# Adaptive max pooling over 8192 rows: a nine-row ring, long load runs, and all stores behind all loads on GpSimd's queue

## The chip, the cores and the metric

The kernel runs on one core of one Trainium2 chip. The metric is the device time of an execution in microseconds (us). A time given as a median is that of several executions; a span is the time from the first to the last instruction of the one execution that the profiler recorded, and is a little shorter than that execution's own time.

## The reference

The input `x` has 32 x 256 x 4096 float32 values, 134.2 MB. Each row of 4096 values is cut into 256 windows of 16, and the largest value of each window is kept. The output has 32 x 256 x 256 values, 8.39 MB.

```python
for i in range(output_size):                 # 256
    start = int(i * length / output_size)    # length 4096: windows of 16
    end = int((i + 1) * length / output_size)
    result[:, :, i] = np.max(x[:, :, start:end], axis=-1)
```

## The kernel before

The 32 x 256 rows are seen as 8192 rows of 16 KB. SBUF has 128 partitions, so 64 rows fall to each partition; below, "a row" of the kernel means one row in each of the 128 partitions, 2.1 MB in and 128 KB out. One instruction of VectorE, a `reduce_max` over the innermost axis, turns a row's 128 x 4096 values into 128 x 256.

**Body.** Two rows at a time are loaded (L80), so that a partition receives one contiguous run of 32 KB. `n_body` is 30 such tiles `t`, in a pool of three buffers (`IN_BUFS`). The loads are issued from SP's queue. Each tile is reduced by two instructions (L83) into an output tile `o` of 128 x 512. The first 14 output tiles are stored as soon as they are made, from ScalarE's queue (L92), in runs of 2 KB. The last 16 tiles of the body are put on a list, `deferred`.

**Tail.** `emit_deferred` (L75) issues stores off that list from SP's queue: six behind the last load of the body, five between the two single-row loads and the chunks, five at the end. Two further rows are loaded one by one (`tr`, L107), and the last two rows are loaded in four chunks each (`tl`, L118), runs of 4 KB, each reduced by its own instruction (L121). ScalarE stores the two output tiles of the tail (L127, L131).

The order of work is the program's order on each queue; the tile framework adds the waits. A load waits until the buffer that it is to fill has been reduced, and a reduction waits until its load has landed. SP works its list off in order, so whatever stands behind a waiting load waits too.

Of the kernel before, what the change touches and what calls it, by code (L numbers as in the profile page):

```python
# [1 line left out]

# [4 lines left out]


@with_exitstack  # L10
def kernel(
    ctx: ExitStack,
    tc: tile.TileContext,
    x: bass.AP,
    output_size: bass.AP,
    out: bass.AP,
):
    nc = tc.nc

    B, C, L = x.shape  # L20
    O = int(output_size)
    assert L % O == 0, (L, O)
    W = L // O

    P = nc.NUM_PARTITIONS

    xf = x.flatten_outer_dims()
    of = out.flatten_outer_dims()
    rows = xf.shape[0]
    assert rows % P == 0  # L30

    fp32 = mybir.dt.float32

    R = 2
    IN_BUFS = 3
    CHUNKS_PER_ROW = 4
    N_CHUNK_ROWS = 2
    N_FULL_ROWS = 2
    DEF_A = 6
    DEF_B = 5  # L40
    DEF_C = 5

    while R > 1 and rows % (P * R) != 0:
        R //= 2
    nprow = rows // P
    nmacro = nprow // R
    n_chunks = CHUNKS_PER_ROW if O % CHUNKS_PER_ROW == 0 else 1
    oc = O // n_chunks

    n_tail_prow = min(N_CHUNK_ROWS + N_FULL_ROWS, nprow)  # L50
    n_chunk_prow = min(N_CHUNK_ROWS, n_tail_prow)
    n_tail_macro = -(-n_tail_prow // R)
    n_body = nmacro - n_tail_macro
    tail_start_prow = n_body * R
    n_defer = min(DEF_A + DEF_B + DEF_C, max(n_body - 1, 0))

    xt = xf.rearrange("(n p r) (o w) -> n p r o w", p=P, r=R, w=W)
    ot = of.rearrange("(n p r) m -> n p (r m)", p=P, r=R)

    in_pool = ctx.enter_context(tc.tile_pool(name="inpool", bufs=IN_BUFS))  # L60
    out_pool = ctx.enter_context(
        tc.tile_pool(name="outpool", bufs=min(nmacro, n_defer + 5))
    )

    out_tiles = {}
    deferred: list[int] = []

    def new_out():
        return out_pool.tile([P, R * O], fp32, tag="out", name="o")

    def emit_deferred(k):
        for _ in range(k):
            if deferred:
                m = deferred.pop(0)
                nc.sync.dma_start(out=ot[m], in_=out_tiles[m])  # L75

    defer_start = n_body - n_defer
    for n in range(n_body):
        t = in_pool.tile([P, R, O, W], fp32, tag="in")
        nc.sync.dma_start(out=t, in_=xt[n])  # L80
        o = new_out()
        for r in range(R):
            nc.vector.reduce_max(  # L83
                out=o[:, r * O : (r + 1) * O],
                in_=t[:, r],
                axis=mybir.AxisListType.X,
            )
        out_tiles[n] = o
        if n >= defer_start:
            deferred.append(n)  # L90
        else:
            nc.scalar.dma_start(out=ot[n], in_=o)  # L92

    emit_deferred(DEF_A)

    o = None
    last_n = nmacro - 1
    for q in range(tail_start_prow, nprow):
        n, r = divmod(q, R)
        if r == 0 or o is None:  # L100
            o = new_out()
            out_tiles[n] = o
        if q == nprow - n_chunk_prow:
            emit_deferred(DEF_B)
        if q < nprow - n_chunk_prow:
            tr = in_pool.tile([P, 1, O, W], fp32, tag="inrow", bufs=2)
            nc.sync.dma_start(out=tr, in_=xt[n][:, r : r + 1])  # L107
            nc.vector.reduce_max(  # L108
                out=o[:, r * O : (r + 1) * O],
                in_=tr[:, 0],  # L110
                axis=mybir.AxisListType.X,
            )
        else:
            for c in range(n_chunks):
                tl = in_pool.tile(
                    [P, oc, W], fp32, tag="inchunk", bufs=2 * n_chunks
                )
                nc.sync.dma_start(  # L118
                    out=tl, in_=xt[n][:, r, c * oc : (c + 1) * oc, :]
                )  # L120
                nc.vector.reduce_max(  # L121
                    out=o[:, r * O + c * oc : r * O + (c + 1) * oc],
                    in_=tl,
                    axis=mybir.AxisListType.X,
                )
        if r == R - 1 and n != last_n:
            nc.scalar.dma_start(out=ot[n], in_=o)  # L127

    emit_deferred(len(deferred))

    nc.scalar.dma_start(out=ot[last_n], in_=out_tiles[last_n])  # L131


# [1 line left out]
_INS = ['x', 'output_size']  # L135
_OUTS = [((32, 256, 256), 'float32')]
#: Inputs that are plain numbers.
_NUMBERS = {'output_size': 256}


# [26 lines left out]
```

## Time and profile before

| | |
|---|---|
| median of 7 executions | 338.76 us (338.42 to 339.2) |
| the profiled execution's own time | 339.2 us |
| its span | 337.4 us |
| VectorE busy | 281.0 us, 70 instructions |
| one row's reduction (L83) | 4414 ns |
| VectorE's idle time before L83, ended by a load | 50.4 us |
| HBM read, written | 134.22 MB, 8.39 MB |
| moved over the span | 423 GB/s |
| DMA transfers | 30 of 4096 KB, 2 of 2048 KB, 8 of 512 KB, 32 stores of 256 KB |

The instruction rows of the profile give the engines' work; the DMA rows give what the 16 DMA engines did. A "packet" of the DMA rows is one contiguous run, as one of the engines moved it, or one of the tiny records with which a transfer reports that it has landed, 16 for each transfer. The share of a queue is the time that its packets took, over 16 engines' span.

### The profile page before, as it was taken

What the parts mean: (1) busy time and instruction counts of PE and PEld (TensorE: products, weight loads), DVE (VectorE), ACT (ScalarE), POOL (GpSimd) and SP (SyncE); (2) the same over time, 40 slices, a digit from 0 to 9 for tenths busy, and PEclk for the clock granted to TensorE, in tenths of its full rate; (3) what the DMA queues carried; (4) which work ended last, traced back from release to release, by engine and by line L of the source; (5) the groups of instructions that cost most, each with busy time, mean ns of one, the idle gap of its engine ahead of it and who ended that gap; (6) DMA issues with size and microseconds to landing.
All of it is one profiled execution on the core that took longest, in us unless ns stands there. A gap on an engine that the chain in (4) does not pass through costs nothing.

```text
span 337.4 us, 241 instructions
## 1 busy us (share of the span) xinstructions
DVE 281.0 (83%) x70; POOL 0.2 (0%) x4
## 2 busy tenths in 40 slices
DVE  0488988888988889888889888888998888899885
POOL 0000000000000000000000000000000000000000
DMA  8999999999999999999999999999999999999997
GB/s 315 435 435 454 404 454 409 450 412 450 418 441 434 426 436 421 458 400 458 404 436 435 435 435 435 435 435 435 431 435 435 435 431 435 417 395 430 400 388 279
DMA packets 10370, 142.63 MB, mean 423 GB/s; under 512 B 1152, under 2 KB 1152, under 8 KB 6272
## 3 DMA queue, kind: packets, MB, share of 16 engines
q1 hardware_dynamic: 8064, 138.42, 96.1%
q10 hardware_dynamic: 2304, 4.20, 3.2%
q14 instruction: 2, 0.02, 0.0%
HBM read 134.22 MB, written 8.39 MB: 423 GB/s over the span
## 4 chain that ended last, share of the span: by engine, by line
DMA 74%; DVE 24%; SPq 1%; issue 0%; DVEq 0%
DMA t<-in_x_dram 60%; DVE o L83 23%; DMA tl<-in_x_dram 7%; DMA out_dram<-o 7%; SPq L75 1%; DVE o L121 0%; SPq L80 0%; DVEq L83 0%
## 5 line engine op out<-in xcount | busy, mean ns | idle before, releaser
L83 DVE TENSOR_REDUCE o<-t 128x256 f32<-128x4096 f32 x60 | 262.4, 4414 | 50.4 <-DMA t<-in_x_dram 50.4
L121 DVE TENSOR_REDUCE o<-tl 128x64 f32<-128x1024 f32 x8 | 9.8, 1220 | 1.2 <-DMA tl<-in_x_dram 1.0
L108 DVE TENSOR_REDUCE o<-tr 128x256 f32<-128x4096 f32 x2 | 8.8, 4420 | 1.3 <-DMA tr<-in_x_dram 1.2
L148 POOL MEMSET const-bfloat16-1.0<- 128x1 bf16 x1 | 0.1, 102 | 0.0
L148 POOL MEMSET const-uint8-127<- 128x1 uint8 x1 | 0.1, 102 | 0.0
L148 POOL MEMSET const-float32-1.0<- 128x1 f32 x1 | 0.1, 99 | 0.0
L148 POOL MEMSET const-float32-0.0<- 128x1 f32 x1 | 0.1, 98 | 0.2 <-issue 0.2
## 6 DMA issues: line engine op xcount, KB each, us to landing
t<-in_x_dram SPq DMA_DIRECT2D x30, 4096.0 KB, 21.6
out_dram<-o ACTq DMA_DIRECT2D x16, 256.0 KB, 15.2
out_dram<-o SPq DMA_DIRECT2D x16, 256.0 KB, 14.3
tr<-in_x_dram SPq DMA_DIRECT2D x2, 2048.0 KB, 16.5
tl<-in_x_dram SPq DMA_DIRECT2D x8, 512.0 KB, 9.4
```

The source lines that it names most:

```text
L75: nc.sync.dma_start(out=ot[m], in_=out_tiles[m])
L83: nc.vector.reduce_max(out=o[:, r * O : (r + 1) * O], in_=t[:, r], axis=mybir.AxisListType.X,)
L108: nc.vector.reduce_max(out=o[:, r * O : (r + 1) * O], in_=tr[:, 0], axis=mybir.AxisListType.X,)
L121: nc.vector.reduce_max(out=o[:, r * O + c * oc : r * O + (c + 1) * oc], in_=tl, axis=mybir.AxisListType.X,)
L148: nc = _bacc.Bacc("TRN2", target_bir_lowering=False, num_devices=1)
```

## The change

The input comes through one tile, `ring`, of nine rows. `LOAD` is three: every load brings three rows, a run of 48 KB in each partition, into a third of the ring; there are 21 of them, and one load of a single row at the end. The rows are dealt out in three groups of `G` = 21 rows to a partition, so that a partition's 21 rows are contiguous in the input and in the output; the runs that the partitions load at one time are thus 336 KB apart. Every row has its own reduction into one of three output tiles of 21 rows (21 KB in each partition); they stay in SBUF until the loads are issued. The last row is reduced into a free part of the ring, `spare`.

After the last load the stores are issued: two whole groups (21 KB runs), the third in two pieces (`CUT`: 15 rows, 6 rows), and the last row's 1 KB runs.

The helper `move` picks the queue. The very first load is issued from SP. All other loads, and four of the five stores, are issued from GpSimd's queue with `single_packet=True`; the last row's store is issued from ScalarE. SP's queue thus holds one transfer, ScalarE's one, GpSimd's 25. On GpSimd's queue the order is: loads 2 and 3, which wait for nothing; loads 4 to 21 and the last row's, each of which waits for an earlier load and for VectorE; the stores of groups 1 and 2 without a wait of their own; the two stores of group 3, each with a wait for VectorE.

```diff
@@ -15,126 +14,78 @@
     output_size: bass.AP,
     out: bass.AP,
 ):
+
+
+
     nc = tc.nc
+    P = nc.NUM_PARTITIONS
+    fp32 = mybir.dt.float32
 
     B, C, L = x.shape
     O = int(output_size)
     assert L % O == 0, (L, O)
     W = L // O
-
-    P = nc.NUM_PARTITIONS
-
     xf = x.flatten_outer_dims()
     of = out.flatten_outer_dims()
     rows = xf.shape[0]
-    assert rows % P == 0
+    assert rows == 64 * P
 
-    fp32 = mybir.dt.float32
+    RING = 9
+    G = 21
+    N_GROUPS = 3
+    LOAD = 3
+    CUT = 15
 
-    R = 2
-    IN_BUFS = 3
-    CHUNKS_PER_ROW = 4
-    N_CHUNK_ROWS = 2
-    N_FULL_ROWS = 2
-    DEF_A = 6
-    DEF_B = 5
-    DEF_C = 5
+    pool = ctx.enter_context(tc.tile_pool(name="pool", bufs=1))
+    ring = pool.tile([P, RING, O, W], fp32, tag="ring", name="ring")
+    outs = [
+        pool.tile([P, G * O], fp32, tag=f"out{i}", name=f"out{i}")
+        for i in range(N_GROUPS)
+    ]
 
-    while R > 1 and rows % (P * R) != 0:
-        R //= 2
-    nprow = rows // P
-    nmacro = nprow // R
-    n_chunks = CHUNKS_PER_ROW if O % CHUNKS_PER_ROW == 0 else 1
-    oc = O // n_chunks
+    main = N_GROUPS * G * P
+    xg = xf[0:main].rearrange("(g p r) (o w) -> g p r o w", p=P, r=G, w=W)
+    og = of[0:main].rearrange("(g p r) m -> g p (r m)", p=P, r=G)
+    xl = xf[main:rows].rearrange("p (o w) -> p o w", w=W)
+    ol = of[main:rows]
 
-    n_tail_prow = min(N_CHUNK_ROWS + N_FULL_ROWS, nprow)
-    n_chunk_prow = min(N_CHUNK_ROWS, n_tail_prow)
-    n_tail_macro = -(-n_tail_prow // R)
-    n_body = nmacro - n_tail_macro
-    tail_start_prow = n_body * R
-    n_defer = min(DEF_A + DEF_B + DEF_C, max(n_body - 1, 0))
+    def pooled(dst, src):
+        nc.vector.reduce_max(out=dst, in_=src, axis=mybir.AxisListType.X)
 
-    xt = xf.rearrange("(n p r) (o w) -> n p r o w", p=P, r=R, w=W)
-    ot = of.rearrange("(n p r) m -> n p (r m)", p=P, r=R)
+    def move(dst, src):
+        if n_read == 0:
+            nc.sync.dma_start(out=dst, in_=src)
+        else:
+            nc.gpsimd.dma_start(out=dst, in_=src, single_packet=True)
 
-    in_pool = ctx.enter_context(tc.tile_pool(name="inpool", bufs=IN_BUFS))
-    out_pool = ctx.enter_context(
-        tc.tile_pool(name="outpool", bufs=min(nmacro, n_defer + 5))
-    )
+    n_read = 0
+    for g in range(N_GROUPS):
+        for r in range(0, G, LOAD):
+            at = n_read % RING
+            move(ring[:, at : at + LOAD], xg[g][:, r : r + LOAD])
+            for i in range(LOAD):
+                pooled(outs[g][:, (r + i) * O : (r + i + 1) * O], ring[:, at + i])
+            n_read += LOAD
 
-    out_tiles = {}
-    deferred: list[int] = []
+    at = n_read % RING
+    spare = ring[:, (at + LOAD) % RING].rearrange("p o w -> p (o w)")[:, 0:O]
+    move(ring[:, at], xl)
+    pooled(spare, ring[:, at])
 
...
+    for g in range(N_GROUPS - 1):
+        move(og[g], outs[g])
+    for a, b in ((0, CUT), (CUT, G)):
+        move(
+            og[N_GROUPS - 1][:, a * O : b * O],
+            outs[N_GROUPS - 1][:, a * O : b * O],
+        )
+    nc.scalar.dma_start(out=ol, in_=spare)
```

More of the change, by code (lines that the diff above doesn't have):

```diff
@@ L66 @@
-    deferred: list[int] = []
[L68 to L90, printed above, removed]
-        else:
-            nc.scalar.dma_start(out=ot[n], in_=o)
@@ L94 @@
[L94 to L127, printed above, removed]
@@ L129 @@
-    emit_deferred(len(deferred))
-    nc.scalar.dma_start(out=ot[last_n], in_=out_tiles[last_n])
+    assert rows == 64 * P
[12 more added lines that the diff above has]
+    xg = xf[0:main].rearrange("(g p r) (o w) -> g p r o w", p=P, r=G, w=W)
```

## The prediction

> **What bounds the kernel now.** I read the page's busy shares and DMA queues first, then the waits, then the DMA view in windows.
>
> ```profile
> span 337.4 us, 241 instructions
> DVE 281.0 (83%) x70; POOL 0.2 (0%) x4
> q1 hardware_dynamic: 8064, 138.42, 96.1%
> q10 hardware_dynamic: 2304, 4.20, 3.2%
> L83 DVE TENSOR_REDUCE o<-t 128x256 f32<-128x4096 f32 x60 | 262.4, 4414 | 50.4 <-DMA t<-in_x_dram 50.4
> ```
>
> The two queues' packets (SP is q1, ScalarE q10) took 99.3% of 16 engines' span: the 16 DMA engines are the bound. VectorE needs 4.41 us a row of tiles and all its 50.4 us of idle time at L83 ended with a load. A row is 2.10 MB, 4.85 us at the 432 GB/s that the table of windows gives for 14 to 300 us; so VectorE keeps pace with 9% to spare.
>
> Time can therefore come only from what DMA records cost, from gaps between them, and from the two ends. Three windows of the DMA view give the price of a record. 200 to 260 us (32 KB load records only), 309 to 315 (16 KB only), 60 to 70 (loads with ScalarE's 2 KB stores):
>
> ```profile
> q1 hardware_dynamic: 889, 25.99, 100.5%
> ...
> q1 hardware_dynamic: 174, 2.59, 101.2%
> ...
> q1 hardware_dynamic: 143, 4.16, 96.4%
> q10 hardware_dynamic: 143, 0.26, 6.8%
> ```
>
> Columns: packets, MB, share of 16 engines. Each transfer also has 16 tiny records (72 transfers, 1152 records under 512 B on the page). First line: 889 - 96 = 793 records in 0.1005 x 600 x 16 = 964.8 us, **1216 ns for 32 KB**. Second: 158 in 97.2 us, 615 ns for 16 KB. Fourth: 127 in 10.9 us less 0.1 for the tiny ones, 84.6 ns for 2 KB. The first and last give a line: **9.2 ns + 36.83 ns per 1000 B** (1131.4 ns over 30,720 B); it puts 16 KB at 612.6, near the measured 615. The tiny ones I take at the line's 9.2.
>
> The last two lines show also how two queues share an engine: 143 records each. They take turns one for one, whatever their size.
>
> Now add up the records of one engine (an eighth of 128 partitions' runs, 8 a transfer): 240 of 32 KB, 291.8; 16 of 16 KB, 9.8; 64 of 4 KB at 160, 10.2; 256 of 2 KB, 21.7; 72 tiny, 0.7. **Sum 334.2.** The DMA view shows the first bytes near 1.76 us and the last near 336.2, 1.2 before the end: 1.76 + 334.2 + 1.2 = 337.2 against 337.4. The kernel before is one unbroken row of records, its tail included.
>
> **What the Trainium skill says.** (1) "DMA: Bandwidth & Descriptors", Queues, rings and completion order: an engine goes round its queues packet by packet and drains a whole packet first. The trace agrees on turns, and shows 32 KB records of SP's queue as turns of their own; no packet of several records is in it. (2) Same page, Specifications: first byte some 1 us after issue from GpSimd, 0.6 from SP. SP's took 1.0 here (issue at 0.73). (3) "SBUF — State Buffer", Who interferes with whom: on trn2 a tensor_reduce never contends with GpSimd, so descriptors written by GpSimd aren't held up by VectorE. No run here shows it yet; I cost that contention at nothing. (4) First page again, Latency and other measured facts: engines 7 and 15 are usually slower, perhaps from GpSimd's descriptor rings. The trace, with no GpSimd DMA, can't say.
>
> **The change, part by part.** *Longer records.* An engine's loads become 21 x 8 = 168 records of 49,152 B at 9.2 + 1810.3 = 1819.5 ns, 305.7 us, and 8 of 16 KB, 4.9. The reader should see how little is to be had: bytes cost 36.83 either way, and 240 + 16 + 64 = 320 fixed parts become 176, 144 x 9.2 ns = 1.3 us. *Stores.* Two groups of 21,504 B a partition (801 ns), then 15,360 (575) and 6,144 (235.5), and the last row's 1,024 (46.9): 8 x 2459.4 ns = 19.7 us, for 21.7. *Fewer transfers:* 27 for 72, 0.25 for 0.66 us. **Sum 330.5, 3.7 less**, all of it on the bounding engines: -1.3 - 2.0 - 0.4.
>
> *The ring.* Nine rows in loads of three keep three loads in flight. In the order of instructions a load's reuse waits on VectorE and the earlier load only. Load k+3 can issue 13.24 us (3 x 4.414) after load k lands, while loads k+1 and k+2 hold the engines for 8 x 1819.5 = 14.56 us each. It is then queued 29.1 - 13.2 = 15.9 us ahead of need, less some 1.4 us for GpSimd's issue. Cost nothing, covered by those two loads. If the cover goes, the engines idle.
>
> *Issue from GpSimd.* All but two of 27 transfers go to POOL's queue, which had four memsets. SP keeps load 1, ScalarE the last row's store. Nothing else needs POOL. The trace has no GpSimd DMA: queued records should follow each other as on SP. Bounds for the whole row: 27 gaps of up to 0.1 us, +2.7, and one packet of eight records shedding all the fixed parts but one, 7/8 x 208 x 9.2 ns, -1.7. I take 0, as no row shows either.
>
> *The start.* Loads 2 and 3 wait for nothing and enter beside load 1. By one-for-one turns, load 1, some two records ahead, sends its other six against six of load 2: it ends near 1.76 + 14 x 1.82 = 27.2, and lands by about 28.8 (the first load's 8 records before end by 1.76 + 9.7, and L83 starts at 13.2, 1.7 later). It landed at 13.2 before, so VectorE starts some 15 us later; yet what decides is load 4, which needs 13.2 us of reductions and 1.4 of issue: 43.4, and loads 1 to 3 last until 1.76 + 43.7 = 45.4. **No gap, by 2 us.** So 0. VectorE's backlog then shrinks by 14.56 - 13.24 = 1.3 us a load and costs nothing: 15 us over 20 loads leave none at the end.
>
> *The tail.* All loads are out at 1.76 + 310.6 + 0.2, 312.6; the stores' 19.7 us follow on the same queue. Stores 1 to 3 wait for rows long reduced. Behind the last load stand two waits: the 6,144-byte store needs row 62, the last one the row after. Load 21 lands near 309; 13.2 + 4.4 bring 322.2 and 326.6, with issue 323.6 and 328. The engines reach these stores at 312.6 + 8 x (2 x 0.801 + 0.575) = 330.0. Cover 6.4 and 2.0 us. Were the last row late by more, each us would cost one. Before, the last reduction (L121) also had stores behind it to fill the engines, so nothing is gained there.
>
> *Sum:* 1.76 + 330.5 + 1.2 = 333.5 by the model, which had 337.2 for before: -3.7. The profiled execution took 339.2 us outside its 337.4 span, 0.44 above the median of 338.76. Counted against its own 339.2: 335.5; on the median's level, 338.76 - 3.7 = **335.0** rounded.
>
> **The rivals.** *A, slower: a packet as a turn.* If GpSimd's eight records of 48 KB go as one unbroken turn of 14.56 us, load 1, which alone is SP's and in eight packets, gets a record or two, then waits out load 2, gets one, waits out load 3, and finishes last at 45.4, landing near 47. VectorE starts there, load 4 issues after 13.2 us and reaches the engines at 61.6. They idle 16.2 us with nothing queued, once; later loads are queued in time (load 5 issues 13.2 us after load 4 and has 14.56). 335.0 + 16.2 = **351.2**, 3.7% slower. The point of decision: load 1 landing after 45.4 - 14.6 = 30.8 us; from 34.5 on, the gap exceeds the 3.7 gained. For it: point (1) of the skill, whole packets. Against it: all turns that the trace shows are single records, and that a 384 KB packet is served unbroken is shown nowhere. If GpSimd's start took over 11 us, load 1 would be through, but the page gives no sign of that.
>
> *B, GpSimd's rings slow two engines.* A transfer ends with its slowest engine. Some 200 GpSimd records an engine at 18 ns more each eat up the 3.7 us; at 9 to 35 ns the time is 337 to 342. For it, point (4); against it, descriptors are few, 9 per engine in 14.56 us.
>
> *C, longer records bring nothing*, since each 48 KB is cut up below: at 16 KB pieces, 336 more fixed parts, 3.1 us, and the time is 338.1. Against it: the runs of 32 KB stood as single records.
>
> **How the numbers follow.** A measurement of this kernel tells some 0.2% (0.7 us) from no change. The forecast 0.53, range of its own 333.0 to 337.7 by the bounds of GpSimd's issue (-1.7, +2.7, rounded). A 0.36, 348 to 352. B 0.08, C 0.03. Faster: 0.53 and half of C and a quarter of B, less the forecast's fringe, 0.55. Same 0.03. Slower: A and most of B, 0.42. The two large cases stand on opposite sides, so the range holds both, 333 to 352.
>
> **What would show it.** Right: both queues' shares still near 99%, packets of 48 KB at some 1820 ns, VectorE's first reduction before 31 us, no slice of the DMA row near zero, last store issued about 327. A: the first reduction at 46 to 47 and one hole of some 16 us after it, at 45 to 61. B: mean record times up and no hole. C: more than 3500 load packets. Wrong altogether: holes that recur with each load, which would mean that GpSimd's issue takes longer than the 15.9 us ahead.

## The result, and the profile after

The changed kernel takes 337.63 us (median of 13 executions, 337.13 to 338.77), the kernel before 338.79 (34 executions on the same chips). The ratio is 0.9965, 95% interval 0.9957 to 0.9973: faster by 0.35%, 1.2 us, where 3.7 had been forecast. Run again on another chip it gave 0.9962 (0.9948 to 0.9976). The direction was right; the size was a third of the forecast. The time lies just inside the range given with the forecast, 333.0 to 337.7.

The page of the changed kernel: its span, busy shares, the DMA engines in 40 slices, queues (packets, MB, share of 16 engines), the reductions, and the last store from GpSimd (KB, us from issue to landing):

```profile
span 335.6 us, 158 instructions
DVE 278.1 (83%) x64; POOL 13.5 (4%) x29
...
DMA  9899899999999999999899998999999999999996
...
q0 software_dynamic: 3600, 136.19, 94.1%
q1 hardware_dynamic: 144, 6.29, 4.5%
q10 hardware_dynamic: 144, 0.13, 0.1%
...
L53 DVE TENSOR_REDUCE out<-ring 128x256 f32<-128x4096 f32 x63 | 273.8, 4411 | 48.8 <-DMA ring<-in_x_dram 48.8
...
out_dram<-out POOLq DMA_DIRECT2D x1, 768.0 KB, 10.9
```

q0 is GpSimd's queue, q1 SP's, q10 ScalarE's. The DMA engines still are the bound: 98.7% of 16 engines' span, and 3889 packets where there were 10370. The span is some 1.8 us shorter. The profiled execution took 337.72 us and its span, to two decimals, 335.57, so 2.15 us lie outside the span; before, 339.2 less 337.43 left 1.78.

The DMA view from 3 to 30 us shows how SP's load 1 and GpSimd's load 2 share the engines:

```profile
q0 software_dynamic: 127, 6.24, 53.4%
q1 hardware_dynamic: 127, 5.51, 47.1%
```

They take turns record by record: 127 packets each, although GpSimd's transfer was issued with `single_packet=True`. (SP's 127 are 112 records of 48 KB, by their 5.51 MB, and 15 of the tiny ones that follow them.) The timeline (start, duration, engine, line) shows what follows from it:

```profile
30.68 52.01 DVE L53 TENSOR_REDUCE out<-ring 128x256 f32<-128x4096 f32 x12 [30.68 <-DMA ring<-in_x_dram]
44.05 0.53 POOL L59 DMA_DIRECT2D ring<-in_x_dram  x1 [41.58 <-DVE out L53]
```

VectorE starts at 30.7 us and load 4 is issued at 44.05; no hole of 16 us stands behind load 3. And the DMA view from 100 to 300 us, which holds loads only (224 of its packets are tiny records):

```profile
q0 software_dynamic: 1984, 86.51, 100.2%
```

1760 records of 48 KB in 1.002 x 3200 us, less 2 us for the tiny ones, are 1821 ns each; 1819.5 had been forecast. So the middle of the kernel runs as predicted, and what is missing has to be looked for at the two ends and in the price of what was removed. GpSimd's last store is in the timeline, and the row of the closing line L113 (durations in ns, smallest, median, largest; first and last start in us) shows what GpSimd does behind it. DRAIN is one of the instructions that end the program on an engine's queue; SP's row and GpSimd's row of the kernel before (closing line L162) stand below it:

```profile
322.88 0.53 POOL L59 DMA_DIRECT2D out_dram<-out  x1 [28.54 <-DVE out L53]
```

```profile
L113 POOLq DRAIN  x3: 40/96/11980, 322.9 to 335.3; - x3
L113 SPq DRAIN  x3: 7/7/7, 333.8 to 335.1; - x3
...
L162 POOLq DRAIN  x3: 34/41/75, 0.7 to 337.2; - x3
```

The store lands at 322.88 + 10.9 = 333.8 us. The DRAIN that starts at 322.9 lasts 11.98 us, until 334.8: one microsecond longer than the data. SP, which waits for the landings, is in its own first DRAIN at 333.8; the program's last instructions come only behind GpSimd's. In the kernel before no GpSimd transfer existed, and the longest of the three DRAIN instructions lasted 0.075 us.

### The profile page after: what moved, and what is told of

Same layout as the page of the kernel before. It is cut to its first block, busy times and chain, and to the rows that moved or that the text cites. A ratio compares the mean times of both kernels' runs of the same rounds, so it can differ in the third digit from the quotient of the medians.

```text
span 335.6 us, 158 instructions
## 1 busy us (share of the span) xinstructions
DVE 278.1 (83%) x64; POOL 13.5 (4%) x29
## 2 busy tenths in 40 slices
DMA packets 3889, 142.62 MB, mean 425 GB/s; under 512 B 432, under 2 KB 560, under 8 KB 688
## 4 chain that ended last, share of the span: by engine, by line
DVE 49%; DMA 45%; DVEq 2%; issue 0%
DVE out L53 48%; DMA ring<-in_x_dram 45%; DVEq L113 2%; DVE ring L53 1%
## 5 line engine op out<-in xcount | busy, mean ns | idle before, releaser
L53 DVE TENSOR_REDUCE out<-ring 128x256 f32<-128x4096 f32 x63 | 273.8, 4411 | 48.8 <-DMA ring<-in_x_dram 48.8
L59 POOL DMA_DIRECT2D ring<-in_x_dram x21 | 11.2, 534 | 274.0 <-DVE out L53 273.2
L53 DVE TENSOR_REDUCE ring<-ring 128x256 f32<-128x4096 f32 x1 | 4.4, 4411 | 0.0
L59 POOL DMA_DIRECT2D out_dram<-out x4 | 2.1, 534 | 35.6 <-DVE out L53 35.6
## 6 DMA issues: line engine op xcount, KB each, us to landing
out_dram<-out POOLq DMA_DIRECT2D x1, 768.0 KB, 10.9
```

The costliest lines, as they stand in the source:

```text
L53: nc.vector.reduce_max(out=dst, in_=src, axis=mybir.AxisListType.X)
L59: nc.gpsimd.dma_start(out=dst, in_=src, single_packet=True)
```

## The experiments

All are timed beside the kernel before, whose medians on the chips used were 338.6 to 338.8 us. The first question was whether issue from GpSimd had cost something, and whether its flag had.

**Everything from SP.**

```diff
-        if n_read == 0:
-            nc.sync.dma_start(out=dst, in_=src)
-        else:
-            nc.gpsimd.dma_start(out=dst, in_=src, single_packet=True)
+        nc.sync.dma_start(out=dst, in_=src)
```

> The changed kernel with every load and the four stores issued from SP instead of GpSimd; nothing else differs. Theory D (GpSimd's drain): the changed kernel ended 1.07 us after its last landing because GpSimd's DRAIN, which began at 322.9 us, ended only at 334.8; without GpSimd transfers the end follows the landing by 0.2 us as before, some 0.9 us are saved, and the records of 48 KB stay at 1815 ns: 336.3 to 336.9 us. Rival P (packets): issue from GpSimd as one packet saves something on the records or between them, and without it the time is 337.6 or more. Rival M (memory pattern): the missing gain is in loads 10 to 14, which lasted 14.6 us instead of 14.5; if that comes from the 336 KB spacing, these loads are as long here.

Measured 335.93 us, ratio 0.9918 (0.9905 to 0.9932). Faster than any theory had it: 2.8 us below the kernel before on the same chip, and 1.7 below the change's median, which was not taken beside it. Rival P falls, and so does M: the records of the DMA view from 100 to 300 us took 1820 ns on average, and none of loads 10 to 14 stood out (nor did they when the changed kernel was run again). GpSimd's longest DRAIN on the closing line is back at 0.070 us:

```profile
L110 POOLq DRAIN  x3: 34/41/70, 0.7 to 334.0; - x3
```

Outside the span lie 1.78 us, as before the change. That is why the gain is more than the drain's.

**Only the third group's store from SP, and whole.** The other loads and two groups' stores stay with GpSimd.

```diff
-    for a, b in ((0, CUT), (CUT, G)):
...
+    nc.sync.dma_start(out=og[N_GROUPS - 1], in_=outs[N_GROUPS - 1])
```

> The changed kernel with the third group stored whole, in one transfer from SP's queue, so that GpSimd's last transfer is the second group's store; loads and the rest as in the change. Theory D: GpSimd's drain ends while SP's store still moves, so its 0.9 us fall away and the time is 336.5 to 337.0 us. Rival: the drain follows whatever landed last, or the end has another cause: 337.4 to 337.9. GpSimd's row should show the DRAIN ending about 2 us or more before SP's last wait.

Measured 335.9 us, ratio 0.9918 (0.9905 to 0.9932), the same as with everything on SP though 23 transfers still come from GpSimd. The closing line's row in this kernel:

```profile
L109 POOLq DRAIN  x3: 34/90/42790, 285.7 to 333.9; - x3
```

GpSimd goes into its DRAIN at 285.7, right behind its last issue, and leaves it at 328.5, while SP's store (issued at 322.2, 11.0 us to landing) moves until 333.2. By the trace's landing events the last of the 23 transfers had landed at 327.5, so the drain again ended 1.0 us behind; it is as real as before, and covered. The time is below the 336.5 to 337.0 expected, since here too only 1.77 us lie outside the span (335.98 less 334.21).

**Without the flag.**

```diff
-            nc.gpsimd.dma_start(out=dst, in_=src, single_packet=True)
+            nc.gpsimd.dma_start(out=dst, in_=src)
```

> The changed kernel without single_packet=True. The trace of the changed kernel showed SP's first load and GpSimd's second taking turns record by record, so one packet was no unbroken turn. My theory: the flag does nothing to the time, 337.3 to 337.9 us, with the same turns and 1815 ns a record. Rival P: the flag is what makes GpSimd's records as cheap as SP's; without it each record, or each transfer, costs more, and 200 records an engine at 10 to 30 ns more give 339.6 to 343.6.

Measured 337.23 us, ratio 0.9958 (0.9946 to 0.9971), which the change's own interval overlaps; just under the time expected, and 1.3 us above the version on SP, timed on the same chip. The DMA view from 3 to 30 us has the same turns:

```profile
q0 software_dynamic: 127, 6.24, 53.4%
q1 hardware_dynamic: 128, 5.55, 47.5%
```

The flag does nothing here that a measurement can tell.

**One GpSimd transfer at the end of the kernel before.**

```diff
-    nc.scalar.dma_start(out=ot[last_n], in_=out_tiles[last_n])
+    nc.gpsimd.dma_start(out=ot[last_n], in_=out_tiles[last_n])
```

> The kernel before with its very last store (L131) issued from GpSimd instead of ScalarE; one GpSimd transfer in all. Theory D: the drain behind one late GpSimd transfer adds its 0.9 us, and GpSimd's slower issue 0.2 to 0.5 more where nothing covers it: 339.7 to 340.4 us. If the drain's price grows with the number of transfers, it is 0.1 us here and the time is 338.8 to 339.3. Rival: no drain cost at all, 338.8.

Measured 338.95 us, ratio 1.0008 (1.0000 to 1.0017). A fixed drain price of 0.9 us is excluded; that was my first form of the theory. The store was issued at 333.92; its landing and the closing line's row:

```profile
out_dram<-o POOLq DMA_DIRECT2D x1, 256.0 KB, 2.4
...
L162 POOLq DRAIN  x3: 34/88/2518, 333.9 to 336.9; - x3
```

The store landed after 2.4 us, and the DRAIN took 2.5, 0.1 us more.

So the next question: does the drain grow with the number of transfers?

**One GpSimd transfer at the end of the version on SP.** The store of the third group is whole, and GpSimd's only transfer.

> All loads and the first two groups' stores from SP; the third group stored whole from GpSimd, so that the last transfer but ScalarE's is GpSimd's and is the only one it ever issued. Theory D by count (the drain takes some 43 ns for each transfer that GpSimd issued in the whole program, 1.07 us for 25, 0.08 for one): 335.9 to 336.3 us, DRAIN ending 0.1 us after its landing. Rival, a fixed price for a late GpSimd transfer, 1.07 us and 0.4 outside the span: 337.2 to 337.6.

Measured 335.93 us, ratio 0.9920 (0.9906 to 0.9933). The two rows, from the timeline and from the closing line:

```profile
322.23 0.66 POOL L74 DMA_DIRECT2D out_dram<-out  x1 [321.78 <-DVE out L53]
```

```profile
L108 POOLq DRAIN  x3: 34/88/10813, 322.2 to 333.8; - x3
```

Landing took 10.7 us, the DRAIN 10.8; it was over at 333.0, before ScalarE's last store landed (326.3 + 6.8 = 333.1). One late transfer from GpSimd costs nothing that shows.

**One row a load, from SP and from GpSimd.** In both, `LOAD` is 1; in the first all is on SP, in the second the queues are the change's, and GpSimd issues 67 transfers.

```diff
-    LOAD = 3
+    LOAD = 1
```

> Everything on SP as in the run with all transfers there, but each load brings one row: 64 loads in runs of 16 KB for 22, so 336 more load records an engine and 42 more tiny ones. By the price of the prediction, 9.2 ns for a record's fixed part, 3.1 and 0.4 us more than 335.9: 339.2 to 339.6 us. Rival: the length of the runs matters more than the fixed part (page or row effects of the memory), or not at all: over 341, or below 337.

Measured 339.53 us, ratio 1.0021 (1.0012 to 1.0030): 3.6 us above the same kernel with three rows a load. Over 336 more load records and 42 more tiny ones an engine that is 9.5 ns each. The prediction's price of a load record's fixed part, 9.2 ns, holds.

> The changed kernel with one row a load: 67 transfers from GpSimd for 25. Theory D by count: the records cost what they cost from SP, and the drain after the last landing grows from 1.07 to some 2.9 us, the part outside the span from 0.4 to about 1.0: 3.5 to 4.2 us above the same loads from SP, near 343. Rival, a fixed price: 1.5 to 1.9 us above them, near 341.

Measured 342.02 us, ratio 1.0097 (1.0083 to 1.0111): 2.5 us above the same loads from SP. The last store, in the timeline and among the DMA issues, and the closing line:

```profile
317.03 0.53 POOL L59 DMA_DIRECT2D out_dram<-out  x1 [23.23 <-DVE out L53]
```

```profile
out_dram<-out POOLq DMA_DIRECT2D x1, 768.0 KB, 19.5
```

```profile
L113 POOLq DRAIN  x3: 40/96/22349, 317.0 to 339.8; - x3
```

It lands at 336.5; the DRAIN ends at 317.0 + 22.35 = 339.4, **2.8 us later**. With one transfer it was 0.1, with 25 it was 1.1, with 67 it is 2.8: 41 ns for each transfer that GpSimd issued in the program (2.7 over 66). Read in the same way, the landing events and DRAINs of the other traces stand on this line: 0.98 us with 23 transfers, 1.03 with 24, 1.11 with 26 (the last two are kernels that come below). A fixed price is out. The part outside the span was 1.77 us here and did not grow, which makes the total one microsecond less than I expected.

**The first load from GpSimd too.** SP's queue is then empty.

> The changed kernel with its first load from GpSimd as well. Load 1 then has the engines alone and lands near 17.5 us, load 4 is queued 15 us ahead, and the slow first records of loads 4 and 5 (0.3 us over the average engine) should go; GpSimd's first byte comes some 0.7 us later than SP's. My theory: 337.7 to 338.4 us. Rival: the shared start costs more than the trace shows, and the time is 337.0 or less.

Measured 338.04 us, ratio 0.9979 (0.9972 to 0.9987), in the range expected. VectorE starts at 19.1 us instead of 30.7, load 4 is issued at 32.5 instead of 44.05, and it brings nothing, for the DMA view of the first 4 us has its first bytes near 2.7 instead of 1.7 us (issue at 1.3: the 1.4 us that the prediction allowed for GpSimd). Does the shared start of the change cost anything? The DMA view from 45.7 to 62 us, when loads 4 and 5 begin, first of the change, then of this kernel:

```profile
q0 software_dynamic: 176, 7.08, 101.8%
```

```profile
q0 software_dynamic: 175, 7.08, 100.4%
```

Load 4's records last longer in the change, but the same bytes move in the same time. The kernel with only the third group's store on SP has the shared start too, and 102.1% in this window; yet it took 335.9 us, like the version on SP, which had 100.4%. So no price of the start shows in the time, and the slow records that this run was expected to save were not shown to be worth anything.

**The third group whole, from GpSimd; and the change again.** 24 transfers for 25.

> The changed kernel with the third group stored whole from GpSimd: 24 transfers for 25, the last one longer (6.4 us for 1.9) and queued 2.4 us before the engines reach it. Theory D by count: DRAIN ends 1.03 us after the last GpSimd landing, and the time stays at 337.3 to 337.7 us; rival: with the last store whole, as in the run that had it on SP, the loss is gone wherever it is issued, 335.8 to 336.3. What the 0.4 us outside the span belong to is open; they are here or not.

Measured 337.07 us, ratio 0.9958 (0.9945 to 0.9970). It is below the 337.3 to 337.7 expected by 0.2, but far from the rival's 335.8 to 336.3; beside the changed kernel on the same chip it does not differ clearly. Its DRAIN ended 1.03 us behind the last GpSimd landing, as expected.

> The changed kernel once more, unaltered, beside these two on one chip: 337.4 to 337.8 us, DRAIN ending 1.07 us after the last landing. Open is whether the time outside the span is again 2.15 us, where the runs without late GpSimd transfers, and the one with 67 of them, had 1.77.

Measured 337.33 us, ratio 0.9962. Outside the span were 2.16 us, so that part recurs; in the 14 executions of the changed kernel with a recorded span it was 2.1 to 2.2 in each. The DRAIN again ended 1.07 us behind the landing.

That leaves 0.9 us of the shortfall, which the version on SP has as well (2.8 gained for 3.7). The load term holds, so the store term was next.

**Short stores.** All on SP; each group is stored in runs of two rows.

```diff
-    for g in range(N_GROUPS - 1):
-        move(og[g], outs[g])
...
+    for g in range(N_GROUPS):
+        for a in range(0, G, 2):
+            b = min(a + 2, G)
+            move(og[g][:, a * O : b * O], outs[g][:, a * O : b * O])
```

> Everything on SP as in the run with all transfers there, but the three groups are stored in runs of 2 KB (two rows), all behind the last load: 33 stores for 4, 264 store records an engine for 32. Theory S: the prediction priced a store record by its duration (84.6 ns), but stores standing back to back overlap, and one takes 80 to 82 ns of the engine's time; so the records cost some 0.9 us more than the long ones and their 29 x 9 ns of tiny ones 0.2: 336.9 to 337.2 us, for 335.9. Rival, the prediction's price: 2.1 and 0.3 us more, 338.2 to 338.5.

Measured 339.46 us, ratio 1.0024 (1.0014 to 1.0034), above both theories, and for another reason. The DMA row from 327 to 331 us, and the wait of SP's queue (line, released by, us in total, times, longest):

```profile
DMA  9941599830111000000000000000058999999999
```

```profile
SPq L56 <- DMA out_dram<-ring: 3.4, 1, 3.4
```

The engines stand still because a store of SP's queue waits for ScalarE's store to land: with so many transfers the two had come to share a semaphore (107 in the trace). It says nothing on the price of a record. The same with the last row's store from SP as well:

> The run with short stores again, with the last row's store from SP too. Before, ScalarE's store and SP's shared a semaphore, SP's queue waited for ScalarE's landing, and the engines stood idle for some 2 us from 328 on; that hole is no price of short records. Theory S, 80 to 82 ns for a store record standing in a row: 336.9 to 337.3 us, no hole in the DMA row behind the last load. Rival, 84.6 ns and 9 more for the tiny ones: 338.2 to 338.5.

Measured 337.2 us, ratio 0.9953 (0.9941 to 0.9965), within theory S. The DMA view from 314 to 332 us, stores only, without a hole:

```profile
DMA  9999999999999999999999999999999999999999
...
q1 hardware_dynamic: 4086, 7.19, 104.6%
```

The durations of the records add up to more than the time: they overlap. Long stores bring 1.3 us over short ones (337.2 less 335.93; by the ratios 0.9953 and 0.9918, 1.2), where the prediction's prices give 2.4 (29 transfers fewer among them). Against the kernel before, on the same chip, this kernel gained 1.4 us (338.64 less 337.2), and there the prices give 1.3: the loads' 1.3 and 16 transfers fewer. So the shortfall lies, within the intervals of some 0.4 us, in the step from short to long stores.

## Why the prediction was right or wrong

**Bound, ring, reductions: right.** The queues' share stayed near 99%, GpSimd's issue of 0.53 us kept the engines fed (100.2% from 100 to 300 us), and VectorE's reductions took 4.41 us beside it. That a tensor_reduce does not hold up GpSimd's descriptors, as the Trainium skill has it ("SBUF — State Buffer", Who interferes with whom), agrees with the trace: the 19 loads issued from 44 us on, with VectorE mostly busy, took 0.53 us each, as load 3 did while VectorE stood idle.

**Longer records: right.** 1821 ns for 1819.5; and 9.5 ns for a fixed part of 9.2 by the loads of one row.

**The start: right in the price, with luck in the margin.** The first reduction came at 30.7 us, before the 31 given, but 1.9 later than the 28.8 worked out. Load 1's data were through at 28.5 in the trace, not 27.2, and the last of its tiny records followed at 30.3, 1.8 us later. That is as long as one 48 KB record, so the tiny records seem to have taken their turn behind records of load 2. The forecast 2 us of slack shrank to almost none: load 4 was issued at 44.05, and 1.4 us later, at about 45.4, load 3 ends by the prediction's count. By that count a few tenths more would have left the engines idle. As it was, no price shows in the time.

**Rival A: fell.** The Trainium skill ("DMA: Bandwidth & Descriptors", Queues, rings and completion order) has an engine drain a whole packet before it turns to the next queue. In this trace a load gave way after every 48 KB record, with the `single_packet` flag and without it; whether the flag makes one packet of a load at all, no run here shows. Rivals B and C fell too. With 23 transfers from GpSimd the kernel took as long as with none (335.9 us), where B needs 1.8 us or more; and 48 KB runs stand as single records (1760 in the window above). B's "some 200" records are right; the 208 in the lower bound for one packet should be 200 as well, which changes -1.7 to -1.6.

**The step that failed is the end of the sum.** "1.76 + 330.5 + 1.2" carried the kernel before's 1.2 us from last byte to last instruction over to the change. There it was 2.2 (last bytes at 333.4 in the trace, end of the span at 335.6): with 25 transfers on GpSimd its DRAIN ends 1.1 us behind the landing, where a landing had taken 0.2 to be acted upon, some 0.9 us more. "Nothing else needs POOL" counted the instructions before the end and missed the one behind them. In the same step, 2.15 us instead of 1.78 lie outside the span: 0.4 us. Together that is 1.3 us, and 1.3 us lie between the change without its flag and the version on SP, timed on one chip (337.23 less 335.93). The changed kernel's own median is 1.7 above; the last 0.4 did not recur in full, for run again it was 337.33, with the kernel before at 338.61.

**The second error is the store term.** It took 84.6 ns, a record's duration, for what a record costs. Stores of 2 KB standing in a row overlap: where their durations make 104.6% of the time, one takes 84.6 / 1.046 = 81 ns. So what the prediction's prices put at 2.4 us, for long store records and fewer transfers, was worth 1.2 to 1.3. That the overlap is the same where stores stand between loads, as the first 14 of the kernel before do, is not shown. The prediction's model had met the span of the kernel before within 0.2 us, which seemed to confirm every price; with a store term about a microsecond too high, something else must have been too low. What, was not separated (slow first records and the lag of the slowest engine are candidates).

In sum: -1.3 for loads (as forecast) and -1.3 for stores and fewer transfers (for -2.4), together near the 2.8 gained with everything on SP; +1.3 for what GpSimd adds; about -1.4, where -1.2 was measured (-1.3 when run again, -1.5 without the flag). That the time still lies inside the range of 333.0 to 337.7 is luck: the 2.7 us at its upper end were for gaps between GpSimd's transfers, and there were none (1821 ns a record).

**Left open:** what the 0.4 us outside the span are. They were there in the change, twice, without the flag, with 24 transfers (2.05) and with the first load on GpSimd (2.04); not with 67 transfers of one row (1.77), nor where GpSimd finished early or issued one transfer. Open too is what the DRAIN does, and whether it counts transfers or runs: each transfer here moved 128 runs.

The best version is the one on SP, or equally the change with its third group stored from SP: 335.9 us, 0.8% faster than the kernel before.

## What to carry to other kernels

An engine's queue has an end: when transfers are moved to another queue, look at what that queue still does after its last transfer, and let a queue without such work carry the last one. Here that was worth 1.3 us. Price a record that stands in a row by the distance between records, not by its duration; shares above 100% in the DMA view show the difference. And a model that meets the span is no proof of its terms; change one term alone before relying on it.

## What the runs showed of the hardware that was not expected

- GpSimd's closing DRAIN ends later than its last landing by 41 ns for each transfer of 128 runs that it issued: 0.1 us for one, 1.1 for 25, 2.8 for 67. Where another queue's last transfer lands later, this is covered.
- A load issued from GpSimd with `single_packet=True` takes turns with another queue after each 48 KB record, here 127 packets to 127 from 3 to 30 us, as it does without the flag.
- The tiny records that report a landing seem to take their turn too: the last of load 1's ended at 30.3 us, its last data at 28.5, and 1.8 us are as long as one 48 KB record of the other queue.
- Stores of 2 KB standing in a row overlap; their durations add up to 104.6% of the time.
